# Rotary embedding over slabs of 4 MB: the first four slabs loaded as two halves of 64 partitions through two DMA rings

## The chip, the cores and the metric

The kernel runs on one NeuronCore of a Trainium2 chip. The metric is device time in microseconds (us) for one execution. Before the change the median of three runs is 162.21 us (162.07 to 162.32). The engines are called as the profile calls them: PE is TensorE, DVE is VectorE, ACT is ScalarE, POOL is GpSimd, SP is SyncE. A DMA is issued by an engine into that engine's own ring: in this kernel SP's ring is queue q1 in the profile, ACT's is q10 and POOL's is q0. All rings are served by the same 16 DMA engines.

## What is computed

```python
x = x.reshape(batch, seq, num_heads, head_dim)      # 16, 512, 16, 64, float32
x1, x2 = x[..., :half_dim], x[..., half_dim:]       # half_dim = 32
cos = cos[None, :, None, :]                         # 512 x 32
sin = sin[None, :, None, :]
rotated = np.concatenate([x1 * cos - x2 * sin,
                          x1 * sin + x2 * cos], axis=-1)
```

x is 33.5 MB and so is the result, both float32 in HBM; the two tables are 64 KB each. Every element is read once, rotated against its partner in the same head, and written once.

## The kernel before

The batch is cut into 8 *slabs* of two batch entries, 4 MB each. A slab lies in the SBUF as 128 partitions of 8 rows of 1024 values: one partition holds 8192 float32, 32 KB, which are contiguous in HBM. Five buffers (`slots = 5`, pool `slabs`) hold slabs, so slabs 0 to 4 can be loaded at once and slab s + 5 needs the buffer of slab s, after its store has read it. The result of a slab is written over its input in the same buffer.

`load(s)` (line 60) allocates a buffer and issues one DMA of 128 partitions (line 64): through SP's ring for slabs 0 to 5, through POOL's ring for slabs 6 and 7. Slab 0's load is the first thing in the program; the loads of slabs 1 to 4 stand at line 81, the others are called at line 150 right after the store that frees their buffer.

The cos and sin tables are loaded into the tile `raw` (lines 73 to 78) through ACT's ring, 32 rows of 2 KB each, into every fourth partition; the tile is set to zero first, one half by DVE and one by POOL. POOL casts them to bf16 (`tab1`, line 97), PE spreads them over the 128 partitions with eight small matmuls against a selection matrix (`pick`, `acc`, line 104), and DVE copies the result from PSUM into `tab` (line 110). `tab` holds for each partition the factors of its rows. No rotation can begin before `tab` is there.

The work on a slab is done in passes: one pass for slabs 1 to 5, two half passes for slabs 0, 6 and 7. A pass has five steps:

- ACT casts the slab's rows to bf16 (`cast`, line 119, into one of two buffers `xb`).
- DVE multiplies them by the sin factors (line 140, `t2`, written into the slab's own buffer, whose input is no longer needed).
- DVE multiplies them by the cos factors (line 140, in `xb`).
- DVE adds the two with the halves of each head swapped (line 143).
- ACT casts the sum back to float32 into the slab's buffer (line 146).

After a slab's last pass ACT issues its store (line 148) into ACT's ring. ACT runs its instructions in a fixed order, which the scheduler of the framework sets from the program's order and its own estimates; the cast of the next pass stands ahead of the cast back of this one in the program (line 134). In the built kernel before, ACT's order begins: the two table DMAs, the load of its activation table, the two half casts of slab 0, the cast of slab 1, the two half casts back of slab 0, the store of slab 0, the cast of slab 2, the cast back of slab 1, the store of slab 1, and so on. SP holds only the six loads. POOL holds the preparation of the tables and the loads of slabs 6 and 7.

Of the kernel before, what the change touches and what calls it, by code (L numbers as in the profile page):

```python
# [2 lines left out]

# [4 lines left out]


@with_exitstack  # L10
def kernel(
    ctx: ExitStack,
    tc: tile.TileContext,
    x: bass.AP,
    cos: bass.AP,
    sin: bass.AP,
    num_heads: int,
    out: bass.AP,
):
    nc = tc.nc  # L20
    P = nc.NUM_PARTITIONS

    batch, seq, dim = x.shape
    nh = num_heads
    hd = dim // nh
    half = hd // 2
    bf16 = mybir.dt.bfloat16
    f32 = mybir.dt.float32

    nb = 2  # L30
    slots = 5
    nslabs = batch // nb
    rpp = nb * seq // P
    W = rpp * dim
    SP = seq // rpp
    TW = rpp * half

    out_flat = out.rearrange("b s h d -> b s (h d)")

    singles = ctx.enter_context(tc.tile_pool(name="singles", bufs=1))  # L40
    slabs = ctx.enter_context(tc.tile_pool(name="slabs", bufs=slots))
    xpool = ctx.enter_context(tc.tile_pool(name="xpool", bufs=2))
    psum = ctx.enter_context(tc.tile_pool(
        name="psum", bufs=1, space=bass.MemoryType.PSUM))


    def dram(t, s, a=0, n=W):
        return bass.AP(tensor=t.tensor, offset=t.offset + s * nb * seq * dim + a,
                       ap=[[W, P], [1, n]])


    def view(t, offset, *dims):
        return dataclasses.replace(t, offset=t.offset + offset,
                                   ap=[t.ap[0], *[list(d) for d in dims]])


    slab = {}


    def load(s):  # L60

        queue = nc.sync if s < nslabs - 2 else nc.gpsimd
        slab[s] = slabs.tile([P, W], f32, tag="slab", name="slab")
        queue.dma_start(out=slab[s], in_=dram(x, s))  # L64


    load(0)


    KQ = 32  # L70
    QS = seq // KQ
    raw = singles.tile([P, 2 * QS * half], f32, tag="raw")
    for i, (eng, src) in enumerate(((nc.vector, cos), (nc.gpsimd, sin))):
        part = raw[:, i * QS * half:(i + 1) * QS * half]
        eng.memset(part, 0.0)  # L75
        nc.scalar.dma_start(out=part[::P // KQ, :], in_=bass.AP(
            tensor=src.tensor, offset=src.offset,
            ap=[[QS * half, KQ], [1, QS * half]]))

    for s in range(1, slots):  # L80
        load(s)


    NQ = QS // rpp
    pick = singles.tile([P, 2 * NQ * P], bf16, tag="pick")
    nc.gpsimd.memset(pick, 0.0)  # L86
    for g in range(2):
        for q in range(NQ):
            part = view(pick, (g * NQ + q) * P + q, (SP, P // SP), (NQ, KQ))
            nc.gpsimd.affine_select(  # L90
                out=part, in_=part, compare_op=mybir.AluOpType.not_equal,
                fill=1.0 - 2.0 * g, base=0,
                pattern=[[0, P // SP], [-(P // KQ), KQ]], channel_multiplier=1)

    tab1 = singles.tile([P, 2 * QS * half], bf16, tag="tab1")
    for i in range(2):
        nc.gpsimd.tensor_copy(out=view(tab1, i * QS * half, (1, QS * half)),  # L97
                              in_=view(raw, i * QS * half, (1, QS * half)))

    acc = psum.tile([P, 2 * rpp * hd], f32, tag="acc")  # L100
    for i in range(2):
        for h in range(2):
            for q in range(NQ):
                nc.tensor.matmul(  # L104
                    view(acc, i * rpp * hd + h * half, (hd, rpp), (1, half)),
                    view(pick, (i * h * NQ + q) * P, (1, P)),
                    view(tab1, i * QS * half + q * TW, (half, rpp), (1, half)),
                    start=q == 0, stop=q == NQ - 1)
    tab = singles.tile([P, 2 * rpp * hd], bf16, tag="tab")
    nc.vector.tensor_copy(out=tab, in_=acc)  # L110

    xb = {}


    def cast(u):
        s, r, n = u
        if r == 0:
            xb[s] = xpool.tile([P, W], bf16, tag="xb", name="xb")
        nc.scalar.copy(out=view(xb[s], r * dim, (1, n * dim)),  # L119
                       in_=view(slab[s], r * dim, (1, n * dim)))  # L120

    passes = []
    for s in range(nslabs):
        n = rpp if 1 <= s < nslabs - 2 else rpp // 2
        passes += [(s, r, n) for r in range(0, rpp, n)]


    cast(passes[0])
    for i, (s, r, n) in enumerate(passes):
        if i + 1 < len(passes):
            cast(passes[i + 1])
        xs = view(slab[s], r * dim, (1, n * dim))
        xu = view(xb[s], r * dim, (1, n * dim))

        t2 = view(slab[s].bitcast(bf16), 2 * r * dim, (1, n * dim))
        for t, a in ((t2, rpp * hd), (xu, 0)):
            nc.vector.tensor_mul(  # L140
                out=t, in0=xu,
                in1=view(tab, a + r * hd, (hd, n), (0, nh), (1, hd)))
        nc.vector.tensor_add(  # L143
            out=xu, in0=xu, in1=view(t2, half, (hd, n * nh), (-half, 2), (1, half)))

        nc.scalar.copy(out=xs, in_=xu)  # L146
        if r + n == rpp:
            nc.scalar.dma_start(out=dram(out_flat, s), in_=slab[s])  # L148
            if s + slots < nslabs:
                load(s + slots)  # L150


# [1 line left out]
_INS = ['x', 'cos', 'sin', 'num_heads']  # L154
_OUTS = [((16, 512, 16, 64), 'float32')]

_NUMBERS = {'num_heads': 16}


# [26 lines left out]
```

## Time and profile before

| | |
|---|---|
| median of 3 runs | 162.21 us (162.07 to 162.32) |
| the profiled execution | 162.06 us, of which the span of its instructions is 160.3 us |
| DVE busy | 109.0 us (68% of the span), 35 instructions |
| ACT busy | 113.6 us (71%), 23 instructions |
| POOL busy | 4.4 us (3%) |
| PE busy | 1.9 us (1%) |
| DMA moved | 67.24 MB in 2400 packets, mean 420 GB/s over the span |
| by queue | q10 (ACT's ring) 1248 packets, 33.69 MB; q1 (SP's) 864, 25.17 MB; q0 (POOL's) 288, 8.39 MB |
| a store, issue to landing | median 26.8 us, from 15.0 to 37.9 |
| a slab's load, issue to landing | 12.8 to 62.3 us |
| the longest waits of engines | POOL's loads for the stores that free the buffers, 84.0 us; ACT's casts for loads, 23.6 us; DVE for ACT's casts, 15.3 us |

Times are read from one execution that the hardware profiler recorded. In the tables of the page each engine's span is cut into 40 slices and a digit gives the busy share of a slice in tenths, 9 being 90% or more. The DMA row is the mean over the 16 DMA engines. In a line of the timeline the columns are start, duration, engine, line of the kernel, operation, tiles, number of instructions, and in brackets the idle time before it with what ended that. A name such as ACTq stands for an engine's instruction stream where it issues a DMA.

### The profile page before, as it was taken

How to read it: one execution, taken by the hardware profiler on the slowest of the kernel's cores; microseconds unless marked ns; L12 is line 12 of the kernel's file. 1: busy time of each engine (PE TensorE's matmuls, PEld its weight loads, DVE VectorE, ACT ScalarE, POOL GpSimd, SP SyncE). 2: the span in 40 equal slices, each digit the busy share in tenths (PEclk: the TensorE clock that was granted, in tenths of full speed). 3: DMA queues.
4: the chain of work that ended last, by engine and by line, in shares of the span. 5: the costliest groups of instructions: out<-in, count | busy, mean ns of one | idle time of the engine just before them, and what ended most of it. 6: DMA issues, size and time to landing. Idle time of an engine off the chain costs nothing.

```text
span 160.3 us, 174 instructions
## 1 busy us (share of the span) xinstructions
PE 1.9 (1%) x8; PEld 1.1 (1%) x8; DVE 109.0 (68%) x35; ACT 113.6 (71%) x23; POOL 4.4 (3%) x14
## 2 busy tenths in 40 slices
PE   0004000000000000000000000000000000000000
PEld 0002000000000000000000000000000000000000
DVE  1000999999989979997996199939559599910000
ACT  3006939998998999899909995199995999280000
POOL 5002000000000000000010001000000000000000
DMA  7999999999999999999999999999999999999994
GB/s 245 417 418 393 499 417 393 474 433 401 384 401 417 474 417 393 474 442 393 458 458 393 450 466 393 433 474 401 417 458 433 393 474 442 393 458 458 393 450 204
DMA packets 2400, 67.24 MB, mean 420 GB/s; under 512 B 288, under 2 KB 288, under 8 KB 352
## 3 DMA queue, kind: packets, MB, share of 16 engines
q10 hardware_dynamic: 1248, 33.69, 48.7%
q1 hardware_dynamic: 864, 25.17, 37.4%
q0 software_dynamic: 288, 8.39, 12.1%
HBM read 33.69 MB, written 33.55 MB: 419 GB/s over the span
## 4 chain that ended last, share of the span: by engine, by line
DMA 49%; ACT 29%; issue 6%; DVE 4%; ACTq 0%; SPq 0%; POOLq 0%
DMA slab<-in_x_dram 28%; DMA out_dram<-slab 21%; ACT slab L146 16%; ACT xb L119 13%; DVE xb L143 1%; DVE xb L140 1%; DVE slab L140 1%; ACTq L148 0%; SPq L64 0%; POOLq L181 0%; ACTq L146 0%; POOLq L64 0%
## 5 line engine op out<-in xcount | busy, mean ns | idle before, releaser
L119 ACT CAST xb<-slab 128x4096 bf16<-128x4096 f32 (+1 forms) x11 | 56.6, 5155 | 24.9 <-DMA slab<-in_x_dram 23.6
L146 ACT CAST slab<-xb 128x4096 f32<-128x4096 bf16 (+1 forms) x11 | 56.6, 5153 | 3.5 <-DVE xb L143 3.5
L140 DVE TENSOR_TENSOR slab<-xb,tab 128x4096 bf16<-128x4096 bf16 (+1 forms) x11 | 35.9, 3260 | 15.4 <-ACT xb L119 15.3
L143 DVE TENSOR_TENSOR xb<-xb,slab 128x4096 bf16<-128x4096 bf16 (+1 forms) x11 | 35.9, 3261 | 0.3
L140 DVE TENSOR_TENSOR xb<-xb,tab 128x4096 bf16<-128x4096 bf16 (+1 forms) x11 | 35.9, 3261 | 0.3
L110 DVE CAST tab<-acc 128x1024 bf16<-128x1024 f32 x1 | 1.2, 1224 | 14.7 <-PE acc L104 14.7
L64 POOL DMA_DIRECT2D slab<-in_x_dram x2 | 1.2, 608 | 84.0 <-DMA out_dram<-slab 84.0
L119 ACT ACT_TABLE_LOAD x1 | 1.3, 1283 | 2.5 <-POOL pick L90 2.5
L104 PE MATMUL acc<-tab,pick 128*128 128x256 bf16 x8 | 1.9, 411 | 14.2 <-POOL tab L97 14.2
L97 POOL CAST tab<-raw 128x512 bf16<-128x512 f32 x2 | 1.2, 611 | 10.9 <-DMA raw<-in_cos_dram 10.9
L104 PEld LDWEIGHTS <-pick 128*128 128x128 bf16 x8 | 1.1, 136 | 14.5 <-issue 12.0
L75 DVE MEMSET raw<- 128x512 f32 x1 | 0.5, 485 | 0.9 <-PEq L167 0.9
L90 POOL TENSOR_SCALAR_AFFINE_SELECT pick<-pick 128x64 bf16<-128x64 bf16 x4 | 0.8, 250 | 0.1
L75 POOL MEMSET raw<- 128x512 f32 x1 | 0.5, 524 | 0.3 <-POOLq L167 0.3
L86 POOL MEMSET pick<- 128x512 bf16 x1 | 0.5, 525 | 0.0
L167 POOL MEMSET const-float32-0.0<- 128x1 f32 x1 | 0.1, 98 | 0.2 <-issue 0.2
L167 POOL MEMSET const-bfloat16-1.0<- 128x1 bf16 x1 | 0.1, 101 | 0.0
L167 POOL MEMSET const-uint8-127<- 128x1 uint8 x1 | 0.1, 101 | 0.0
L167 POOL MEMSET const-float32-1.0<- 128x1 f32 x1 | 0.1, 98 | 0.0
## 6 DMA issues: line engine op xcount, KB each, us to landing
out_dram<-slab ACTq DMA_DIRECT2D x8, 4096.0 KB, 26.8
slab<-in_x_dram SPq DMA_DIRECT2D x6, 4096.0 KB, 27.1
slab<-in_x_dram POOLq DMA_DIRECT2D x2, 4096.0 KB, 23.7
raw<-in_sin_dram ACTq DMA_DIRECT2D x1, 64.0 KB, 8.4
raw<-in_cos_dram ACTq DMA_DIRECT2D x1, 64.0 KB, 11.6
```

Source lines behind the costliest of these rows:

```text
L64: queue.dma_start(out=slab[s], in_=dram(x, s))
L75: eng.memset(part, 0.0)
L86: nc.gpsimd.memset(pick, 0.0)
L90: nc.gpsimd.affine_select(out=part, in_=part, compare_op=mybir.AluOpType.not_equal, fill=1.0 - 2.0 * g, base=0, pattern=[[0, P // SP], [-( ...
L97: nc.gpsimd.tensor_copy(out=view(tab1, i * QS * half, (1, QS * half)), in_=view(raw, i * QS * half, (1, QS * half)))
L104: nc.tensor.matmul(view(acc, i * rpp * hd + h * half, (hd, rpp), (1, half)), view(pick, (i * h * NQ + q) * P, (1, P)), view(tab1, i * QS * ...
L110: nc.vector.tensor_copy(out=tab, in_=acc)
L119: nc.scalar.copy(out=view(xb[s], r * dim, (1, n * dim)), in_=view(slab[s], r * dim, (1, n * dim)))
L140: nc.vector.tensor_mul(out=t, in0=xu, in1=view(tab, a + r * hd, (hd, n), (0, nh), (1, hd)))
L143: nc.vector.tensor_add(out=xu, in0=xu, in1=view(t2, half, (hd, n * nh), (-half, 2), (1, half)))
L146: nc.scalar.copy(out=xs, in_=xu)
L167: nc = _bacc.Bacc("TRN2", target_bir_lowering=False, num_devices=1)
```

## The change

For slabs 0 to 3 `load` issues only partitions 0 to 63, through SP's ring; the new function `load_rest` issues partitions 64 to 127 through ACT's ring. For slabs 0 to 2 it is called from `load`, for slab 3 after the first cast. Slab 4 and slab 5 still come whole through SP's ring, slabs 6 and 7 whole through POOL's.

```diff
+    H = P // 2
+
     def load(s):
         queue = nc.sync if s < nslabs - 2 else nc.gpsimd
         slab[s] = slabs.tile([P, W], f32, tag="slab", name="slab")
-        queue.dma_start(out=slab[s], in_=dram(x, s))
+        if s < slots - 1:
+            queue.dma_start(out=slab[s][:H, :], in_=dram(x, s)[:H, :])
+            if s < slots - 2:
+                load_rest(s)
+        else:
+            queue.dma_start(out=slab[s], in_=dram(x, s))
+
+    def load_rest(s):
+        nc.scalar.dma_start(out=slab[s][H:, :], in_=dram(x, s)[H:, :])
...
     cast(passes[0])
+    load_rest(slots - 2)
     for i, (s, r, n) in enumerate(passes):
```

In the built kernel ACT's order now begins: slab 0's upper half, the cos table, the sin table, the upper halves of slabs 1 and 2, the load of the activation table (which now waits for slab 0's upper half), the first half cast of slab 0, slab 3's upper half, the second half cast of slab 0, the first half cast back of slab 0, the cast of slab 1, the second half cast back, the store of slab 0. The first half cast back and the cast of slab 1 have changed places; from the store of slab 0 on ACT's order is the old one. SP's order is the lower halves of slabs 0 to 3, then slabs 4 and 5; the lower half of slab 3 waits for the completion of slab 0's lower half and slab 4 for that of the cos table, whose semaphores they use again. DVE, PE and POOL run the same instructions in the same order.

## The prediction

> **What bounds the kernel now.** I read the busy slices and transfer rates of the page first, then the same rates by stage, then the order of work on the engines.
>
> ```profile
> DVE  1000999999989979997996199939559599910000
> ACT  3006939998998999899909995199995999280000
> DMA  7999999999999999999999999999999999999994
> ...
> DMA packets 2400, 67.24 MB, mean 420 GB/s; under 512 B 288, under 2 KB 288, under 8 KB 352
> ```
>
> The DMA row is at 9 from the second slice to the last but one, while VectorE and ScalarE have holes. The queues never drain. How little is lost shows by stage (columns: stretch, its length, busy time of five engines, clock, DMA share, GB/s):
>
> ```profile
> 1.20:3.20 2.00, 0.00 (x0) 0.10 (x1) 0.20 (x1) 0.69 (x1) 1.35 (x6) 1.00 0.95 262
> 3.20:37.20 34.00, 1.86 (x8) 0.99 (x7) 20.88 (x9) 21.74 (x6) 1.17 (x2) 1.00 1.01 435
> 37.20:61.40 24.20, 0.00 (x0) 0.00 (x0) 22.67 (x6) 23.37 (x4) 0.00 (x0) 1.00 0.99 413
> 61.40:84.40 23.00, 0.00 (x0) 0.00 (x0) 21.85 (x6) 18.44 (x3) 0.69 (x1) 1.00 1.00 433
> ...
> 144.40:158.00 13.60, 0.00 (x0) 0.00 (x0) 0.00 (x0) 0.02 (x1) 0.00 (x0) 1.00 1.01 436
> 158.00:160.30 2.30, 0.00 (x0) 0.00 (x0) 0.00 (x0) 0.00 (x0) 0.00 (x0) 1.00 0.00 0
> ```
>
> 433 GB/s is the ceiling, for loads alone (435), loads beside stores (433) and stores alone (436). At it, 67.24 MB take 155.3 us of the 160.3 us span. The other 5 us: about 1.7 us until the first packets move, 0.7 us while they come up to speed, 0.9 us in a dip near 41 us (262 GB/s from 40 to 42 us, where store 0 joins; it is why the stage from 37.2 us has only 413), and 1.3 us after the last data. **So only the 1.6 us of ramp and dip can be won in the middle, and every microsecond in which all queues stand empty is lost.**
>
> The second fact is how two rings share the engines:
>
> ```profile
> DMA packets 48, 1.57 MB, mean 315 GB/s; under 512 B 0, under 2 KB 0, under 8 KB 0
> ...
> q1 hardware_dynamic: 48, 1.57, 86.8%
> ```
>
> ```profile
> q1 hardware_dynamic: 112, 3.15, 101.2%
> q10 hardware_dynamic: 96, 0.13, 4.9%
> ```
>
> The first is from 1 to 6 us, the second from 6 to 13.2 us. Queue q1 is SyncE's ring with slabs, q10 ScalarE's with the two tables. In the second stretch each of 16 DMA engines passes 7 slab packets (112/16) and 6 small ones: one of each in turn. A table needs three turns (two rows and its completion), so it takes 3.8 us however small it is: sin landed at 1.29 + 8.4 = 9.7 us, cos at 1.87 + 11.6 = 13.5 us.
>
> **The change, part by part.** *Bytes.* The same 67.24 MB; four more DMAs with their completions cost nothing beside 1.2 us slab packets (a 32 KB row at 433/16 = 27 GB/s).
>
> *The tables move behind half of slab 0.* ScalarE now issues slab 0's upper half, then cos, sin, the upper halves of slabs 1 and 2, then the first cast, then slab 3's half. Slab 0's two halves take turns and carry the bytes that SyncE's ring carried alone, so slab 0 lands at 13.4 us as before. Only then come the tables, six turns beside slab 1's lower half: 13.2 + 2 x 3.8 = 20.8 us instead of 13.5. These are the lines that follow from it:
>
> ```profile
> 13.56 1.17 POOL L97 CAST tab<-raw 128x512 bf16<-128x512 f32 x2 [10.94 <-DMA raw<-in_cos_dram]
> 13.61 7.11 ACT L119 CAST xb<-slab 128x4096 bf16<-128x4096 f32 x2 [9.81 <-DMA slab<-in_x_dram]
> ...
> 17.44 2.29 DVE L140 TENSOR_TENSOR slab<-xb,tab 128x4096 bf16<-128x4096 bf16 x1
> ...
> 23.16 7.02 ACT L119 CAST xb<-slab 128x8192 bf16<-128x8192 f32 x1 [2.44 <-DMA slab<-in_x_dram]
> ...
> 30.09 7.11 ACT L146 CAST slab<-xb 128x4096 f32<-128x4096 bf16 x2
> ...
> 37.23 0.35 ACTq L148 DMA_DIRECT2D out_dram<-slab  x1
> ...
> 51.58 0.34 ACTq L148 DMA_DIRECT2D out_dram<-slab  x1
> ```
>
> VectorE begins 3.95 us after the last table; one table's cast (0.6 us) is now done early, so 20.8 + 3.4 = 24.2 us instead of 17.44.
>
> *ScalarE's order.* The table load (1.28 us) now waits for slab 0's upper half, so the first cast runs from 14.8 instead of 13.6 us; slab 3's half is issued behind it (0.35 us). Both are hidden, since VectorE waits for the tables until 24.2. In the built order the first cast back (line 146) stands ahead of slab 1's cast, where it stood behind it. It waits for VectorE's first pass, which ended 9.0 us after VectorE's start (24.18 + 2.28 - 17.44): 33.2. Then, in ScalarE's order, cast back 3.6 (36.8), slab 1's cast 7.0 (43.8), cast back 3.6 (47.4): store 0 at 47.5 instead of 37.23. VectorE has slab 1 from 43.8 and takes 3 x 4.45 us (57.2); its cast back takes 7.0: **store 1 at 64.3 instead of 51.58**.
>
> *SyncE's waits.* Slab 3's lower half waits for the completion of slab 0's (they share a semaphore), slab 4 for cos's, about 13 and 17 us. Behind them stands only the load of slab 5, which waits for store 0 anyway. The ring still holds slabs 1 and 2's halves (8 turns from 13 us, over 9.7 us), so nothing runs dry.
>
> *Where the stall goes.* Until store 0 is done the engines have slabs 0 to 4, store 0 and the tables: 25.3 MB, 58.4 us at 433, from 1.7 us with 0.7 us of ramp: done at 60.9 us. (ScalarE's ring holds 8.5 MB ahead of store 0, done near 50 us, so store 0 is in time.) Then **all queues are empty**: slab 5 waits for store 0's landing, store 1 for ScalarE until 64.3. Before, store 1 stood in the ring from 51.58 and covered this. Store 0 lands 0.4 us after its last data (the last store: data until 159.1, landed 144.45 + 15.0); SyncE's issue took 1.0 us from 0.74 us to the first packets. So data flow again at 62.4 and ramp for 0.7 us: 1.5 + 0.7 = 2.2 us lost. From there ten transfers of 4.19 MB follow at 9.7 us each. I followed ScalarE on at 14.4 us a slab: stores 2 to 6 near 78.8, 93.2, 107.6, 121.1 and 135.5, the last near 149.5, just ahead of its turn (62.4 + 0.7 + 9 x 9.7 = 150.4); that is 0.9 us of cover where there were 4.9 (159.1 - 9.7 - 144.45), and without it each microsecond counts in full.
>
> *The dip.* Store 0 now follows data in its own ring rather than joining one empty since 13 us. Bounds: 0.9 us won to nothing won. When store 1 followed store 0 (61.4 to 84.4 us, 433 GB/s) no dip is seen, and that is the nearest row, so I take 0.9.
>
> *A transfer of 64 partitions.* No row shows one. Lower bound: as fast as a slab, since 32-row tables already went out to all 16 engines, 16 packets to a turn. Upper bound: half of 433 GB/s, if half the partitions use half of what the engines write through and the rings' halves do not complement each other. The packet time is the same for loads and stores, so the limit does not lie with HBM's direction, which leaves this open. By the nearest row, the tables, I take no loss and keep the upper end.
>
> [...]
>
> **The sum.** +2.2 - 0.9 = +1.3 us on a profiled execution of 162.06 us (span 160.3 and 1.8 around it), 163.4; the median of the runs is 0.15 higher. Slab 0's first rows now come through two rings and the last store has little cover, each worth some tenths, so I say **163.8 us**. Its own range: 162.8 (no ramp at the restart) to 165.3 (dip kept, last store late).
>
> **The rivals.** *Halves at half rate.* Up to 16.8 MB x (1/216 - 1/433) = +38.8 us, 201 us. Slabs 2 and 3's upper halves partly run beside the whole slab 4, which takes some off: about +30, 190 us; if the rings fall into alternation, perhaps +13, 175. For it: each engine's constant 27 GB/s in both directions, which speaks for a limit in the engine or where it meets the SBUF. Against it: the tables' spread.
>
> *The halves keep to eight engines each* (the other side: faster). Whole slabs give each engine eight rows; if a half's 64 rows go to the eight engines that serve them in a whole slab, one ring fills one set and the other the other. The total rate stays 433, and the tables are through right behind slab 0's half, about 13.5 us. VectorE then starts at 18.6 (after the first cast) and store 1 is issued 40.1 us later, at 58.7, ahead of 60.9: no empty queues, and the dip is won: 162.2 - 0.9 = 161.3 us. The deciding point is store 1 before 60 us, so tables by about 16.5. Against it: tables of 32 rows used all engines, though they span all partitions.
>
> *No change.* As the last, but the dip stays: 162.2 us.
>
> **How the numbers follow.** Forecast 0.40, half rate 0.30, eight engines each 0.20, no change 0.10. A measurement of this kernel tells 0.2% (0.3 us) from no change. Slower is the forecast and half rate, 0.70; same 0.10; faster 0.20. The range goes from 161.0 (the gain) to 192 (past the middle of half rate); what lies above is about 0.14, below 0.03.
>
> **What would show it.** Right: tables landing near 21 us, VectorE's first multiply near 24, store 1 near 64, DMA slices at about 61 to 63 us well under 9, no 262 GB/s near 41. Half rate: slab 0 landing near 20 us and 220 to 300 GB/s in the first 40. Eight engines each: tables by 14 us and DMA at 9 throughout. The forecast is wrong if store 1 comes before 60 us or if the first 40 us run below 400 GB/s.

## The result: 203.92 us, and the profile after

The changed kernel takes 203.92 us (median of 6 runs, 202.39 to 204.28) against 162.24: 1.2556 times the kernel before, interval 1.2516 to 1.2595. The profiled execution took 202.39 us with a span of 200.4, 40.1 us more than the 160.3 of before. First the busy slices of the page and the rates below them:

```profile
DVE  0000000099900996699399799229998496991000
ACT  0000285002449609976999990699399969947000
DMA  9999999999999999999999999999999999999994
GB/s 203 209 216 209 209 222 216 209 216 209 209 209 209 262 301 275 249 275 425 445 445 458 419 419 425 419 445 445 464 419 419 425 419 438 445 471 419 419 425 209
```

The DMA engines are as busy as before, and yet they move about 210 GB/s in the first 13 slices (65 us), about 275 in the next five, and the old rate only after that. Here the busy share does not tell the rate: in the stages below it is 0.99 at 213 GB/s and 1.00 at 433. By stage (stretch, length, five engines, clock, DMA share, GB/s), first the kernel before, then the changed one:

```profile
1.20:20.00 18.80, 1.86 (x8) 1.09 (x8) 3.95 (x4) 7.68 (x3) 2.51 (x8) 1.00 1.01 418
20.00:65.00 45.00, 0.00 (x0) 0.00 (x0) 43.37 (x13) 41.73 (x8) 0.00 (x0) 1.00 1.00 422
65.00:92.00 27.00, 0.00 (x0) 0.00 (x0) 21.13 (x6) 22.42 (x5) 0.69 (x1) 1.00 1.00 431
```

```profile
1.20:20.00 18.80, 0.00 (x0) 0.10 (x1) 0.20 (x1) 0.00 (x0) 1.35 (x6) 1.00 1.03 223
20.00:65.00 45.00, 2.03 (x8) 0.95 (x7) 14.88 (x7) 19.03 (x6) 1.23 (x2) 1.00 0.99 213
65.00:92.00 27.00, 0.00 (x0) 0.00 (x0) 23.18 (x6) 17.62 (x4) 0.00 (x0) 1.00 1.00 290
92.00:150.00 58.00, 0.00 (x0) 0.00 (x0) 45.50 (x12) 47.59 (x8) 1.22 (x2) 1.00 1.00 433
```

Against 433 GB/s the first three stages lose 18.8 x (1 - 223/433) = 9.1, 45 x (1 - 213/433) = 22.9 and 27 x (1 - 290/433) = 8.9 us, 40.9 in all. The kernel before loses 1.9 in the same stretches. The difference, 39.0, is the lengthening of the span but for a microsecond. How a packet fares is seen from 6 to 16 us:

```profile
DMA packets 64, 2.10 MB, mean 210 GB/s; under 512 B 0, under 2 KB 0, under 8 KB 0
...
q10 hardware_dynamic: 32, 1.05, 47.7%
q1 hardware_dynamic: 32, 1.05, 47.5%
```

64 packets of 32 KB on 16 engines in 10 us: 2.5 us each, where it was 1.21. Both rings have equal shares and together fill the engines; each packet simply takes twice as long. The rings take turns as a whole: in the trace 16 packets of SyncE's ring and none of ScalarE's start between 8.9 and 11.3 us, and 16 of ScalarE's and none of SyncE's between 11.3 and 13.7. So for most of the time (72% of 5 to 60 us in the trace) packets of one ring alone, and so of one half alone, are under way, up to 16 at once. The work behind it on the engines:

```profile
25.60 3.60 ACT L131 CAST xb<-slab 128x4096 bf16<-128x4096 f32 x1 [3.59 <-DMA slab<-in_x_dram]
...
38.61 0.62 POOL L109 CAST tab<-raw 128x512 bf16<-128x512 f32 x1 [4.62 <-DMA raw<-in_sin_dram]
...
41.64 2.29 DVE L153 TENSOR_TENSOR slab<-xb,tab 128x4096 bf16<-128x4096 bf16 x1
...
68.52 0.35 ACTq L161 DMA_DIRECT2D out_dram<-slab  x1
...
88.95 0.34 ACTq L161 DMA_DIRECT2D out_dram<-slab  x1
```

Slab 0 is there at 25.6 us (13.6 before), the last table at 38.6, store 0 is issued at 68.5. All of it is late, and none of it is the cause: the loads ahead of it set the pace.

### The profile page after: what moved, and what is told of

Its sections match the earlier page's. It is cut to its first block, busy times and chain, and to the rows that moved or that the text cites. A ratio compares the mean times of both kernels' runs of the same rounds, so it can differ in the third digit from the quotient of the medians.

```text
span 200.4 us, 182 instructions
## 1 busy us (share of the span) xinstructions
PE 2.0 (1%) x8; PEld 1.1 (1%) x8; DVE 109.2 (55%) x35; ACT 113.6 (57%) x23; POOL 4.5 (2%) x14
## 3 DMA queue, kind: packets, MB, share of 16 engines
q1 hardware_dynamic: 608, 16.78, 30.3%
## 4 chain that ended last, share of the span: by engine, by line
DMA 37%; ACT 24%; issue 15%; DVE 8%; another core or an unknown queue 7%; POOL 1%; PE 1%; ACTq 0%; POOLq 0%; DVEq 0%
DMA raw<-in_sin_dram 18%; ACT slab L159 14%; DMA slab<-in_x_dram 12%; ACT xb L131 10%; DMA out_dram<-slab 7%; DVE slab L153 2%; DVE xb L156 2%; DVE xb L153 2%; DVE tab L122 1%; PE acc L116 1%; ACTq L161 0%; POOL tab L109 0%; POOL pick L98 0%; POOL pick L102 0%
## 5 line engine op out<-in xcount | busy, mean ns | idle before, releaser
L159 ACT CAST slab<-xb 128x4096 f32<-128x4096 bf16 (+1 forms) x11 | 56.7, 5153 | 19.4 <-DVE xb L156 19.4
L116 PEld LDWEIGHTS <-pick 128*128 128x128 bf16 x8 | 1.1, 132 | 38.8 <-issue 36.3
```

Source lines behind the costliest of these rows:

```text
L116: nc.tensor.matmul(view(acc, i * rpp * hd + h * half, (hd, rpp), (1, half)), view(pick, (i * h * NQ + q) * P, (1, P)), view(tab1, i * QS * ...
```

## The experiments

Theory P: 64 *neighbouring* partitions can only be written at half the rate, whichever ring carries them. Its rivals: two rings of loads together are slow (R), the number of rows or of DMAs (N), the place of the rows in HBM (H).

**One ring.** All eight halves through SyncE's ring.

```diff
-        nc.scalar.dma_start(out=slab[s][H:, :], in_=dram(x, s)[H:, :])
+        nc.sync.dma_start(out=slab[s][H:, :], in_=dram(x, s)[H:, :])
```

> The same eight halves of 64 partitions, but all through SyncE's ring, so that only the tables and the stores use ScalarE's. Theory P (a half's 64 neighbouring partitions can be written at half the rate only, whichever ring carries it): 16.8 MB at about 210 to 217 GB/s, packets of 2.4 us, in place of 433, +39 us: 198 to 202 us. Theory R (two rings of loads at once are what is slow): 162 to 163 us, packets of 1.21 us.

Measured: 210.01 us, 1.2952 times before (1.2931 to 1.2974). From 20 to 40 us one ring alone:

```profile
DMA packets 171, 4.19 MB, mean 210 GB/s; under 512 B 43, under 2 KB 43, under 8 KB 43
...
q1 hardware_dynamic: 160, 4.19, 100.5%
```

128 packets of 32 KB (the other entries are completions) in 20 us on 16 engines: 2.5 us again, with one ring busy. R falls. The time is 8 us over the upper end of what P expected. The rates of the page show where, and the issues of the last three stores why:

```profile
GB/s 189 201 222 208 214 202 202 202 202 202 315 322 341 322 284 246 208 309 429 454 429 410 448 435 423 435 448 429 416 448 435 416 378 448 57 404 404 101 486 221
```

```profile
167.19 0.34 ACTq L159 DMA_DIRECT2D out_dram<-slab  x1
...
181.37 0.34 ACTq L159 DMA_DIRECT2D out_dram<-slab  x1
...
195.54 0.34 ACTq L159 DMA_DIRECT2D out_dram<-slab  x1
```

The loads are over by 160 us, and stores 5, 6 and 7 are issued 14.2 us apart, while a store at 433 GB/s takes 9.7: the queues run empty twice near the end (57 and 101 GB/s), over 4 us each time.

**Halves by columns.** The same rings and order, but each half has all 128 partitions and half of each row.

```diff
-            queue.dma_start(out=slab[s][:H, :], in_=dram(x, s)[:H, :])
+            queue.dma_start(out=slab[s][:, :W // 2], in_=dram(x, s, 0, W // 2))
-        nc.scalar.dma_start(out=slab[s][H:, :], in_=dram(x, s)[H:, :])
+        nc.scalar.dma_start(out=slab[s][:, W // 2:], in_=dram(x, s, W // 2, W // 2))
```

> Halves again, one through each ring in the changed kernel's order, but cut along the columns: 128 partitions x 4096 values, the same 2 MB per DMA. Theory P: full rate, 433 GB/s. Then what the prediction said of the rest can be seen: tables behind slab 0 (packets of 16 KB halve their turns, so 13.2 + 6 x 0.61 = 16.9 us), VectorE's start near 20.3, store 1 near 60.4, empty queues for at most 1 us near 61, no dip near 41: 161.3 to 162.8 us. Theory R, or a cost of many smaller DMAs: 195 us or more.

Measured: 162.35 us, ratio 1.0016 (1.0001 to 1.0032).

```profile
GB/s 180 429 433 424 429 433 437 425 429 429 433 461 425 416 392 490 424 392 482 408 416 449 441 416 425 457 424 400 482 425 392 457 449 400 449 449 408 433 457 155
...
20.25 2.29 DVE L153 TENSOR_TENSOR slab<-xb,tab 128x4096 bf16<-128x4096 bf16 x1
...
58.28 0.35 ACTq L161 DMA_DIRECT2D out_dram<-slab  x1
```

Two rings, the order, later tables and smaller DMAs together cost next to nothing; all but 0.1 of the 41.7 us hang on how the slab is cut. VectorE started at 20.25 us (20.3 expected) and store 1 was issued at 58.3 (60.4).

**Even and odd partitions.** Again 64 rows a half, but every second partition.

```diff
-            queue.dma_start(out=slab[s][:H, :], in_=dram(x, s)[:H, :])
+            queue.dma_start(out=slab[s][::2, :], in_=dram(x, s)[::2, :])
-        nc.scalar.dma_start(out=slab[s][H:, :], in_=dram(x, s)[H:, :])
+        nc.scalar.dma_start(out=slab[s][1::2, :], in_=dram(x, s)[1::2, :])
```

> Halves of 64 partitions through two rings, but the even partitions in one and the odd ones in the other. Theory P: each half then spans all partitions, so the rate should be well above 300 GB/s, and at 433 the prediction's own sum of 163 to 165 us holds. Theory N (it is the number of 64 rows that halves the rate, not which ones): 204 us, packets of 2.4 us.

Measured: 165.88 us, ratio 1.0221 (1.0206 to 1.0236). From 6 to 16 us, the stretch shown above for the changed kernel:

```profile
DMA packets 176, 4.23 MB, mean 423 GB/s; under 512 B 32, under 2 KB 32, under 8 KB 48
```

Twice the bytes, so it is not the number of rows. As the rates are whole here, this run is also the test of everything else in the prediction:

```profile
20.90 0.61 POOL L109 CAST tab<-raw 128x512 bf16<-128x512 f32 x1 [1.91 <-DMA raw<-in_sin_dram]
...
23.93 2.29 DVE L153 TENSOR_TENSOR slab<-xb,tab 128x4096 bf16<-128x4096 bf16 x1
...
28.58 2.29 DVE L156 TENSOR_TENSOR xb<-xb,slab 128x4096 bf16<-128x4096 bf16 x1
...
61.95 0.34 ACTq L161 DMA_DIRECT2D out_dram<-slab  x1
...
63.00 0.33 SPq L72 DMA_DIRECT2D slab<-in_x_dram  x1
```

```profile
60.00:64.00 4.00, 0.00 (x0) 0.00 (x0) 3.97 (x2) 3.54 (x2) 0.00 (x0) 1.00 0.67 287
64.00:72.00 8.00, 0.00 (x0) 0.00 (x0) 6.69 (x2) 8.00 (x2) 0.00 (x0) 1.00 1.05 381
```

The tables are through at 20.9 us and store 1 comes at 61.95. In the trace no packet of data starts between 61.3 us and 62.8, when store 1's first ones do; slab 5's load is issued at 63.0 and its first packets start at 68.2. From 60 to 64 us 4 x (1 - 287/433) = 1.3 us are lost, and 8 x (1 - 381/433) = 1.0 us more as the rings start again.

**Other rows of HBM.** Partitions 0 to 63 from the even rows of the slab, 64 to 127 from the odd ones.

```diff
-            queue.dma_start(out=slab[s][:H, :], in_=dram(x, s)[:H, :])
+            queue.dma_start(out=slab[s][:H, :], in_=dram(x, s)[::2, :])
-        nc.scalar.dma_start(out=slab[s][H:, :], in_=dram(x, s)[H:, :])
+        nc.scalar.dma_start(out=slab[s][H:, :], in_=dram(x, s)[1::2, :])
```

> Partitions 0 to 63 and 64 to 127 as in the changed kernel, but filled from the even and the odd rows of the slab in HBM (so rows come out permuted: the rotation is done on misplaced rows). The HBM side is that of the even and odd halves, the SBUF side that of the changed kernel. Theory P: 202 to 205 us, packets of 2.4 us. Theory H (two neighbouring 2 MB blocks of HBM slow each other): like the even and odd halves.

Measured: 202.84 us in one run.

```profile
GB/s 209 209 209 209 209 222 222 209 209 209 209 209 209 274 294 268 261 261 418 450 470 424 424 418 424 418 470 457 418 424 418 424 437 450 457 424 418 418 424 209
```

HBM's side is that of the even and odd halves, the slowness that of the changed kernel. H falls: what counts is which partitions of the SBUF a half covers.

**Slab 0 alone in halves of 64.** Slabs 1 to 4 whole.

```diff
-        if s < slots - 1:
+        if s < 1:
```

> Only slab 0 is cut into halves of 64 partitions; slabs 1 to 4 come whole through SyncE's ring. Theory P: 4.19 MB at 209 in place of 433 GB/s, 20.1 in place of 9.7 us, so 10.4 us in the slab-0 stage; store 0 and store 1 come late, but all loads end near 61 us and store 1 is issued near 67, before store 0 is through (70): nothing runs empty. 172 to 173.5 us. A fixed cost (some reordering at the start, the same for one slab as for four): far from a quarter of 41.7 us.

Measured: 172.60 us, ratio 1.0634 (1.0617 to 1.0651): +10.4 us for a quarter of the halves, a quarter of 41.7. Rates:

```profile
1.20:20.00 18.80, 0.00 (x0) 0.10 (x1) 0.20 (x1) 0.00 (x0) 1.35 (x6) 1.00 1.03 223
22.00:60.00 38.00, 2.02 (x8) 0.95 (x7) 26.31 (x10) 28.36 (x6) 1.22 (x2) 1.00 0.99 427
```

The rate is back as soon as the halves are through.

**Stores in halves.** The kernel before with the last two stores cut.

```diff
-            nc.scalar.dma_start(out=dram(out_flat, s), in_=slab[s])
+            for a in (0, P // 2):     # slabs 6 and 7 alone
+                nc.scalar.dma_start(out=dram(out_flat, s)[a:a + P // 2, :],
+                                    in_=slab[s][a:a + P // 2, :])
```

> The kernel before, with the stores of slabs 6 and 7 (nothing else is in the queues at the end) cut into halves of 64 partitions on ScalarE's ring. Theory P as a limit of the SBUF side in both directions: 8.39 MB at 209 to 217 in place of 433 GB/s, +19.4 to +20.7 us, 181.5 to 183 us, packets of 2.4 us. A limit for writing into the SBUF alone: 162 to 163 us.

Measured: 179.06 us, ratio 1.1042 (1.1025 to 1.1059): +16.9 us, somewhat less than expected.

```profile
123.00:140.00 17.00, 0.00 (x0) 0.00 (x0) 14.79 (x7) 14.22 (x4) 0.00 (x0) 1.00 1.00 432
141.00:175.00 34.00, 0.00 (x0) 0.00 (x0) 0.00 (x0) 3.52 (x1) 0.00 (x0) 1.00 0.95 217
```

Reading 64 neighbouring partitions is limited as writing them is: 217 GB/s, against 432 before the halves and 213 where the changed kernel loads halves. The shortfall against P's 19.4 us arises chiefly where a half begins: there packets of 1.21 to 2.3 us stand between those of 2.55 (at 139 to 141, 147.6, 155 to 158 and 165 to 167 us in the trace). Why they are faster there is not shown.

**Blocks and spread sets.** The kernel before, slab 0 in pieces of 32 partitions and slab 1 in pieces of 16, once as neighbours, once every fourth and every eighth.

```diff
-        queue.dma_start(out=slab[s], in_=dram(x, s))
+        step = {0: 32, 1: 16}.get(s, P)            # blocks
+        for a in range(0, P, step):
+            queue.dma_start(out=slab[s][a:a + step, :], in_=dram(x, s)[a:a + step, :])
...
+        step = {0: 4, 1: 8}.get(s, 1)              # spread
+        for a in range(step):
+            queue.dma_start(out=slab[s][a::step, :], in_=dram(x, s)[a::step, :])
```

> The kernel before with slab 0 loaded in four blocks of 32 neighbouring partitions and slab 1 in eight blocks of 16, all in SyncE's ring; the rest whole. If the rate goes with the number of partitions covered: 32 partitions a quarter of 433 GB/s (packets of 4.85 us), 16 an eighth (9.7 us), about 260 us in all. [...] If only being under 128 matters: 2.4 us for both, 183 us.

> As the run with blocks of 32 and 16 partitions, with the same numbers of rows and DMAs in the same ring, but spread: slab 0 in four sets of every fourth partition, slab 1 in eight sets of every eighth. If what counts is which partitions are covered: slab 0 at full rate (32 partitions in steps of 4 reach all over the SBUF, packets of 1.21 us), slab 1 at half rate at most (packets of 1.21 to 2.5 us), 162 to 183 us, far under the blocks' 201.8. If the number of rows in a DMA counts: packets of 2.5 and 4.5 us and 202 us again.

Measured: 201.82 us for the blocks, 177.35 for the spread sets, one run each. First the blocks' stages of 32 and of 16 neighbours, then the spread sets' stages of every fourth and of every eighth partition:

```profile
1.20:21.00 19.80, 1.21 (x6) 0.94 (x7) 0.20 (x1) 0.00 (x0) 2.51 (x8) 1.00 1.02 218
21.00:60.00 39.00, 0.65 (x4) 0.15 (x1) 14.71 (x7) 15.60 (x5) 0.00 (x0) 1.00 0.98 125
```

```profile
1.20:12.00 10.80, 1.86 (x8) 1.09 (x8) 0.66 (x2) 0.00 (x0) 2.51 (x8) 1.00 0.99 397
14.00:34.00 20.00, 0.00 (x0) 0.00 (x0) 13.48 (x6) 13.39 (x5) 0.00 (x0) 1.00 0.97 210
```

The same DMAs by count and size, at 218 against 397 GB/s (a stage that includes the start-up) for 32 partitions, and 125 against 210 for 16. The number of partitions alone does not decide (260 us were expected for that), nor does it matter only that a piece is under 128 (183 us): 32 neighbours do as well as 64 neighbours (packets of 2.46 us), 16 do about half of that (4.54 us; the stage's 125 GB/s include some faster packets at its ends), 32 spread ones are not limited (1.21 us), and 16 spread ones come to the rate of 64 neighbours (210 GB/s).

**Engines out of step.** The changed kernel with two extra loads of 8 rows, or of 3, ahead of slab 0 in SyncE's ring, into the bf16 buffers.

```diff
+    for s in range(2):
+        xb[s] = xpool.tile([P, W], bf16, tag="xb", name="xb")
+        nc.sync.dma_start(out=xb[s].bitcast(f32)[:8, :], in_=dram(x, 0, 0, W // 2)[:8, :])
     load(0)
```

> The changed kernel, with two extra loads of 8 rows of 16 KB ahead of slab 0's lower half in SyncE's ring (into buffers that are overwritten later), so that eight of the 16 DMA engines are one packet out of step with the other eight. Theory P in the form of two engines in step on one target (engines e and e + 8 write into the same part of the SBUF at the same time, all on the lower, then all on the upper half): with the two out of step one writes below while the other writes above, packets of 1.2 us come back for part of the first 65 us, and the time falls by 10 us or more, to 175 to 194 us. If instead neighbouring engines share a target, or 64 partitions are limited as a whole: 203 to 206 us, packets of 2.4 us.

> As the run with eight engines out of step, but the two extra loads have 3 rows, so that three of the 16 engines are out of step with the rest. If two engines share one target and neighbours are the partners, the engine of the three whose partner is not among them is freed, with its partner: two engines pass packets in 1.2 us where both work on different halves, all others in 2.4. If the partners are four apart, six engines are freed. If a half of 64 partitions is limited as a whole, whatever the engines do: none under 2.3 us. 198 to 208 us in each case, since a slab waits for its slowest engine; the packets' durations in the first 40 us decide.

Measured: 208.97 us with 8 rows (ratio 1.2896, 1.2864 to 1.2928), 208.11 with 3 (one run). Rates with 8 rows:

```profile
5.00:20.00 15.00, 0.00 (x0) 0.00 (x0) 0.00 (x0) 0.00 (x0) 0.00 (x0) 1.00 1.05 216
20.00:40.00 20.00, 2.02 (x8) 0.97 (x7) 4.04 (x3) 8.39 (x3) 1.22 (x2) 1.00 0.99 208
40.00:65.00 25.00, 0.00 (x0) 0.00 (x0) 15.17 (x6) 14.13 (x3) 0.00 (x0) 1.00 1.01 218
```

The trace's packets do show about eight of one ring starting beside eight of the other for part of the time (from 9.6 to 15.5 us, for one), so that eight engines work on the upper half while eight work on the lower, and with 3 rows three beside thirteen, but not one 32 KB packet between 5 and 40 us took less than 2.3 us. My picture of two engines that meet at one target and are freed when they alternate is refuted in both forms that I tried; the extra loads only cost 4 to 5 us.

**Columns with early tables.** The halves by columns, the tables through GpSimd's ring.

```diff
-        nc.scalar.dma_start(out=part[::P // KQ, :], in_=bass.AP(
+        nc.gpsimd.dma_start(out=part[::P // KQ, :], in_=bass.AP(
```

> Halves by columns through two rings, with the tables loaded through GpSimd's ring instead of behind slab 0's half. The prediction's step of the late tables: with the tables early (by about 14 us) VectorE starts near 18 us, store 1 comes before 60 us, and no queue runs empty: 161.2 to 162.2 us, up to 1 us under the kernel with columns alone. If the tables' place costs nothing at full rate: 162.3 us.

Measured: 164.34 us, ratio 1.0134 (1.0112 to 1.0155), 2 us slower than with columns alone.

```profile
54.98 0.35 ACTq L161 DMA_DIRECT2D out_dram<-slab  x1
```

```profile
50.00:60.00 10.00, 0.00 (x0) 0.00 (x0) 9.93 (x3) 9.52 (x2) 0.00 (x0) 1.00 0.97 419
60.00:70.00 10.00, 0.00 (x0) 0.00 (x0) 8.64 (x3) 9.59 (x3) 0.00 (x0) 1.00 1.01 406
70.00:90.00 20.00, 0.00 (x0) 0.00 (x0) 18.89 (x5) 13.71 (x2) 0.56 (x1) 1.00 1.00 411
```

Store 1 came at 55.0 as wanted, and no queue was empty near 61, but the rates between 60 and 90 us are lower than the 433 of before. Some packets took 1.4 to 2.5 us there in place of 1.21 (at 65.7 to 69 us and 75 to 77); the cause is open. Early tables win nothing, and no version here beats the kernel before.

## Why the prediction was wrong

**The step that failed** is the last of the change's parts: "By the nearest row, the tables, I take no loss". The tables do go out to all 16 engines, and so do the halves (16 packets of one ring at a time); that was no argument. The tables lie in every fourth partition, all over the SBUF, and a half lies in 64 neighbours. The row that I called nearest was near in the number of rows and differed in what counts. In place of "no loss" stand packets of 2.4 to 2.5 us instead of 1.21, 209 to 213 GB/s while the halves run alone, and +41.7 us. At full rate my sum was off by 2.4 us (165.88 us with even and odd halves, +3.7 where I had +1.3).

**What the rate went with.** That both halves share the engines is not the cause: halves by columns share them too, at 162.35 us. Nor does a transfer need all 128 partitions for the full rate: the even and odd halves reached 423 GB/s. The rate went with the partitions that a piece covers: 64 or 32 neighbours 209 and 218 GB/s, 16 neighbours 125, every second or fourth partition 423 and 397, every eighth 210. Why lower and upper half together gained nothing with the engines out of step is not shown.

**The rival "halves at half rate"** had the halved rate, with a chance of 0.30, and too small a loss. I took +30 from an upper end of +38.8; it was +41.7. Both parts were too low. The rate was 209 to 213 and not 216 GB/s: at 209 the halves' bytes alone give 16.78 MB x (1/209 - 1/433) = +41.5 us. And the stage beside the whole slab 4, from which I expected relief, gave none: it ran at 290 GB/s and cost 8.9 us. In the trace (67.5 to 90 us) slab 4's packets took 1.54 us on average instead of 1.21, and the halves' beside them 2.29 instead of 2.43, so that the two took at least as long as one after the other. The smaller number of +13 supposed that the two rings complement each other once they alternate. They do alternate, 16 packets and 16, and gain nothing.

**The rival "eight engines each"** is out: in the changed kernel all 16 engines are at one ring's half at once (from 10.2 to 11.3 us, for one: 16 packets of SyncE's ring under way, none of ScalarE's).

**The other steps**, as the even and odd halves show them: last table 20.9 us (20.8), VectorE's start 23.9 (24.2), store 1 at 61.95 (64.3), a stretch without work near 61, which store 1 ended and not, as I had it, slab 5's load. The 2.3 us in store 1 are my oversight: in the built order VectorE's first add stands third and no longer fourth, so the text on the change, which says that VectorE's order is the old one, is wrong, and pass 0 ended 6.9 us after VectorE's start and not 9.0. The dip of 0.9 us was not won: rates were 415 GB/s from 40 to 60 us and 381 from 64 to 72. So at full rate it was +3.7 us where I had +1.3: a loss near 61 us was rightly forecast (2.3 us in the two stretches above, 2.2 forecast), the credit for the dip was not, and part of the 2.3 is a second dip at the restart that was not in the sum. The other 1.4 us are not assigned to a stage. One reading was wrong without effect: of the 112 entries of SyncE's ring between 6 and 13.2 us, 16 are completions, so an engine passed six slab packets beside six small ones, not seven.

## What to carry to other kernels

Ask of a cut tile which partitions each piece covers, before counting rings, rows or bytes: pieces of neighbouring partitions cut the DMA rate in the loads here from 433 GB/s to 209 to 218 (the lower or upper 64, blocks of 32) or 125 (blocks of 16), the 64 in the stores too (217), and sets of every eighth partition did so as well (210); a cut along the columns (162.35 us in all) or by every second partition (423 GB/s) did not. A whole slab that ran beside such a piece brought no relief, since its packets took longer as well (1.54 us instead of 1.21), so price the piece's bytes at the low rate in full. And where a whole forecast hangs on the nearest row, look for the property in which the row differs from the new operation.

## What was not expected of the hardware

- A DMA engine that is busy all the time can move half the bytes: a 32 KB packet took 1.21 us into a whole slab, 2.4 to 2.5 us into a half of 64 neighbours, and 4.5 us into 16 neighbours.
- Putting engines out of step did not free one packet in the loads (none under 2.3 us), while in the stores by halves packets of 1.21 us came wherever a half began. So what exactly is shared within a half, and by whom, stays open.
- In some runs the rate dipped after a store's ring had started beside loads, by about a microsecond in the kernel before (262 GB/s from 40 to 42 us). Packets of 1.3 to 2.1 us came with even and odd halves too, from 49 to 51 us, and of 1.5 to 1.8 us near 42 us in the run with early tables. The cause was not tried.
